# A decoder layer on one core: the down-projection as seven block products, and the first norm's scale and shift applied to h^T per partition

## The chip, the core and the metric

The kernel runs on one core of a Trainium2 chip. The metric is the device time of one execution in microseconds. Engines are named as in the profile: PE is TensorE, DVE VectorE, ACT ScalarE, POOL GpSimd, SP the engine that issues most of the loads.

## What is computed

One layer of a hybrid decoder over 1024 tokens of width 1024 (float32): a token mixer (a state-space group and a sparse-attention group), an output projection, a first layer norm, a channel mixer, a second layer norm. The part that matters here:

```
h = layer_norm(alpha * x + m, ln1_g, ln1_b)        # m: mixer output after its projection
u = causal_dwconv(h @ w_up, conv_w, conv_b)        # w_up 1024 x 5632, width 3
gate, up = split(u, 2)
f = (silu(gate) * up) @ w_down                     # w_down 2816 x 1024
out = layer_norm(alpha * h + f, ln2_g, ln2_b)
```

## The kernel before, in words

Every product is made of three matmuls (`three`, lines 156 to 159): each operand is split into an upper half (a copy rounded to the fp32r type) and a lower half (the rest), and upper x upper, upper x lower and lower x upper are added in one PSUM bank. The upper half is made by ACT, the lower one by POOL or DVE as `operand - upper` (`split`, lines 125 to 130).

The order on each engine but SP is set by the scheduler of the language, which simulates the program and takes, among the instructions that it expects to be ready, the one that stands first in the text; the engines then run these orders strictly. SP's order is the text's own (line 1134). Buffers are shared by tags with fixed counts (line 73): `wr` 3 (raw weights), `wh` and `wl` 3 each, `t4` 18, `wo` 8, `pp` 8, `pt` 3, `tx` 3; PSUM banks by the tags `ip` 2, `lg` 3, `tp` 2, `pv` 1 (line 75).

*First norm, lines 939 to 976.* For each of 8 token blocks r is loaded (a `pt` buffer), the last part of the output projection is added from PSUM, and `layer_norm` (lines 758 to 773) normalizes it. For the first six blocks (`LNP`, line 42) ACT normalizes, POOL multiplies by the scale (line 766) and DVE adds the shift (767); for the other two DVE does both in four steps (771, 772). The result goes to `h_dr` and is transposed by PE, eight 128 x 128 tiles per block (964). `put` (913 to 918) splits the transposed tile from PSUM into operands of the up-projection: `h11`, `h21` for tokens 0 to 511, `h22`, `t1`, `t2` for tokens 512 to 1023, later `t3`, `t4` (1008 to 1015). The t are differences of blocks of h^T.

*Up-projection, lines 1032 to 1064.* For each of `NF` = 22 column blocks j, seven block products (a Strassen-Winograd scheme over two column blocks, gate and up, two halves of the inner dimension and two halves of the tokens) of 12 matmuls each. `w_prep` (990 to 1005) makes the seven weight operands of the next j: four DVE sums, seven upper halves on ACT, seven lower halves on POOL (1003). Then the convolution (1058 to 1061), Silu and the product of gate and up, and the result goes to `g_dr` (1064).

*Down-projection, lines 1067 to 1109.* For each half of the tokens, eight PSUM banks hold 4 token blocks x 2 column halves. For each of the 22 row blocks k of w_down, `prep` (1074) loads 128 x 1024 of w_down (line 149) and 128 x 512 of g (1079), splits them (ACT 129 and 1080, POOL 130, DVE 1081), and 24 matmuls follow. The last 3 or 4 row blocks (`TAILS`) are run block by block, so that the second norm of one block (DVE, 1108 and `layer_norm`) lies beside the matmuls of the next.

## Time and profile before

| | |
|---|---|
| median of 3 runs | 1762.61 us (1762.0 to 1763.98) |
| profiled execution | 1762.1 us, its span 1760.2 us |
| PE busy in the span | 1622.6 us (92%), 7976 matmuls and transposes |
| DVE, ACT, POOL busy | 1245.4, 841.3, 803.9 us |
| mean granted clock of PE | 0.972 of full speed |
| first norm, up-projection, down-projection | about 1000 to 1085, 1085 to 1501, 1509 to 1760 us |

A busy time is the sum of the instructions' durations on an engine; an instruction's duration includes what it waits for after it has started. PE's matmuls overlap in the records: their pace is read from their starts. Times in rows count from the start of the span.

### The profile page before, as it was taken

What the parts mean: (1) busy time and instruction counts of PE and PEld (TensorE: products, weight loads), DVE (VectorE), ACT (ScalarE), POOL (GpSimd) and SP (SyncE); (2) the same over time, 40 slices, a digit from 0 to 9 for tenths busy, and PEclk for the clock granted to TensorE, in tenths of its full rate; (3) what the DMA queues carried; (4) which work ended last, traced back from release to release, by engine and by line L of the source; (5) the groups of instructions that cost most, each with busy time, mean ns of one, the idle gap of its engine ahead of it and who ended that gap; (6) DMA issues with size and microseconds to landing.
All of it is one profiled execution on the core that took longest, in us unless ns stands there. A gap on an engine that the chain in (4) does not pass through costs nothing.

```text
span 1760.2 us, 22843 instructions
## 1 busy us (share of the span) xinstructions
PE 1622.6 (92%) x7976; PEld 1342.8 (76%) x7976; DVE 1245.4 (71%) x2289; ACT 841.3 (48%) x1495; POOL 803.9 (46%) x560
## 2 busy tenths in 40 slices
PE   7899977888998989999999885999999999899998
PEld 6788866766887767778888764888888888688886
DVE  3534799998689667777787479888788786515516
ACT  3243474676411466666676344444444443333231
POOL 3223224453355443545464357765555553445351
PEclk9999999998999999999999997999999999899999
DMA  5122122123332473545454451322222223446443
GB/s 166 50 67 66 53 64 65 61 78 90 117 96 75 144 216 102 162 133 142 131 160 151 149 171 57 96 85 84 85 84 84 90 74 112 136 147 232 155 147 128
DMA packets 180937, 198.21 MB, mean 113 GB/s; under 512 B 12003, under 2 KB 136279, under 8 KB 180823
## 3 DMA queue, kind: packets, MB, share of 16 engines
q1 hardware_dynamic: 147351, 145.37, 28.0%
q10 hardware_dynamic: 33472, 51.39, 8.0%
q8 instruction: 63, 1.03, 0.3%
q14 instruction: 51, 0.42, 0.1%
HBM read 145.28 MB, written 51.45 MB: 112 GB/s over the span
## 4 chain that ended last, share of the span: by engine, by line
PE 44%; DVE 6%; DMA 2%; ACT 2%; issue 1%; POOL 1%; SPq 0%; DVEq 0%; ACTq 0%; POOLq 0%
PE acc L157 5%; PE acc L158 5%; PE acc L159 4%; PE pc L157 2%; PE pd L157 2%; PE pd L158 2%; PE pc L158 2%; PE pa L157 2%; PE pd L159 2%; PE pc L159 2%; PE ops L158 2%; PE ops L157 2%; PE ops L159 2%; PE pa L158 2%; PE pa L159 2%; PE ptp L695 2%
## 5 line engine op out<-in xcount | busy, mean ns | idle before, releaser
L130 POOL TENSOR_TENSOR w_lo<-w_raw,w_hi 128x1024 fp32r<-128x1024 f32 (+1 forms) x89 | 221.9, 2499 | 162.5 <-ACT w_hi L129 160.2
L157 PE MATMUL proj<-xTh,w_hi 128*128 128x512 f32 (+1 forms) x432 | 175.5, 407 | 30.2 <-DVE conv L483 10.4
L158 PE MATMUL proj<-xTl,w_hi 128*128 128x512 f32 (+1 forms) x432 | 173.7, 402 | 0.0
L159 PE MATMUL proj<-xTh,w_lo 128*128 128x512 f32 (+1 forms) x432 | 172.9, 401 | 0.0
L1003 POOL TENSOR_TENSOR w_hl<-s,w_hl 128x512 fp32r<-128x512 f32 x88 | 129.5, 1476 | 81.2 <-ACT w_hl L1002 80.8
L689 POOL TENSOR_SCALAR prob<-prob,sm 128x512 f32<-128x512 f32 (+7 forms) x128 | 97.5, 772 | 144.6 <-DVE sm L688 114.0
L1081 DVE TENSOR_TENSOR g_hl<-g_raw,g_hl 128x512 fp32r<-128x512 f32 x44 | 59.3, 1354 | 133.7 <-ACT g_hl L1080 129.3
L1003 POOL TENSOR_TENSOR w_hl<-w_raw,w_hl 128x512 fp32r<-128x512 f32 x66 | 106.3, 1613 | 88.9 <-ACT w_hl L1002 58.5
L157 PE MATMUL acc<-w_hi,g_hl 128*128 128x512 f32 x352 | 136.3, 395 | 7.8 <-ACT g_hl L1080 7.8
L158 PE MATMUL acc<-w_lo,g_hl 128*128 128x512 f32 x352 | 137.5, 391 | 0.0
L159 PE MATMUL acc<-w_hi,g_hl 128*128 128x512 f32 x352 | 137.4, 390 | 0.0
L127 POOL TENSOR_SCALAR w_hi<-w_raw 128x1024 fp32r<-128x1024 f32 x35 | 40.8, 1167 | 185.2 <-PE proj L158 153.6
L157 PEld LDWEIGHTS proj<-xTh,w_hi 128*128 128x128 f32 (+1 forms) x432 | 83.5, 193 | 50.6 <-issue 30.5
L686 ACT ACTIVATE prob<-prob,mx 128x512 f32<-128x512 f32 (+7 forms) x128 | 98.5, 771 | 39.2 <-DVE mx L683 36.0
L697 ACT ACTIVATE pt<-ptp 128x512 fp32r<-128x512 f32 x144 | 81.2, 594 | 65.4 <-PE ptp L695 44.6
L698 DVE TENSOR_TENSOR pt<-ptp,pt 128x512 fp32r<-128x512 f32 x144 | 95.5, 685 | 15.5 <-ACT pt L697 15.2
L157 PE MATMUL ops<-w_hi,y_hi 128*128 128x512 f32 x256 | 102.4, 401 | 4.1 <-ACT y_hi L129 3.1
L157 PE MATMUL tps<-w_hi,xTh 128*128 128x256 f32 x320 | 95.9, 301 | 9.6 <-ACT tout L617 6.9
L353 ACT ACTIVATE junk<-score,cand 128x1024 bf16<-128x1024 f32 (+2 forms) x96 | 86.1, 897 | 35.8 <-DVE cand L367 26.1
L158 PE MATMUL ops<-w_lo,y_hi 128*128 128x512 f32 x256 | 101.4, 396 | 0.4 <-DVE w_lo L130 0.4
L159 PE MATMUL ops<-w_hi,y_lo 128*128 128x512 f32 x256 | 100.5, 397 | 0.4 <-POOL y_lo L130 0.4
L129 ACT ACTIVATE w_hi<-w_raw 128x1024 fp32r<-128x1024 f32 (+1 forms) x62 | 65.2, 1052 | 74.0 <-PE acc L159 53.2
(315 smaller groups left out, 4793.3 us busy)
## 6 DMA issues: line engine op xcount, KB each, us to landing
w_raw<-in_ffn_w_up_dram SPq DMA_DIRECT2D x44, 512.0 KB, 3.9
w_raw<-in_ffn_w_down_dram SPq DMA_DIRECT2D x44, 512.0 KB, 3.7
w_raw<-in_w_in_dram SPq DMA_DIRECT2D x36, 512.0 KB, 4.1
r_dr<-rout ACTq DMA_DIRECT2D x48, 256.0 KB, 2.1
g_dr<-vg ACTq DMA_DIRECT2D x22, 512.0 KB, 2.6
g_raw<-g_dr SPq DMA_DIRECT2D x44, 256.0 KB, 4.0
acsb<-a_dr SPq DMA_DIRECT2D x16, 512.0 KB, 4.1
w_raw<-in_w_out_dram SPq DMA_DIRECT2D x16, 512.0 KB, 4.2
```

The lines of the kernel that those rows point to most:

```text
L129: nc.scalar.activation(hi, raw, AF.Copy)
L130: (nc.vector if lo_on_dve else nc.gpsimd).tensor_tensor(lo, raw, f(hi), op=OP.subtract)
L157: nc.tensor.matmul(ps, ah, bh, start=start, stop=False, skip_group_check=onto)
L158: nc.tensor.matmul(ps, ah, bl, start=False, stop=False, skip_group_check=onto)
L159: nc.tensor.matmul(ps, al, bh, start=False, stop=stop, skip_group_check=onto)
L353: nc.scalar.activation(junk[1][:, :n], score_ap[b], AF.Sign, bias=c, scale=-1.0, accum_out=val[e][:, i:i + 1])
L686: nc.scalar.activation(t[:, :w], t[:, :w], AF.Exp, bias=mx[:, h:h + 1], scale=-1.0, accum_out=sm[:, h:h + 1])
L689: nc.gpsimd.tensor_scalar(t[:, :w], t[:, :w], sm[:, 4 + h:5 + h], 1.0, op0=OP.mult, op1=OP.mult)
L697: nc.scalar.activation(pt[:, 0], ps, AF.Copy)
L698: nc.vector.tensor_tensor(pt[:, 1], ps, f(pt[:, 0]), op=OP.subtract)
L1003: nc.gpsimd.tensor_tensor(t[:, 1], src, f(t[:, 0]), op=OP.subtract)
L1081: nc.vector.tensor_tensor(t[:, 1], raw, f(t[:, 0]), op=OP.subtract)
```

## The change

The first norm leaves out scale and shift in the row layout: DVE normalizes r in one `tensor_scalar`, the bare result goes to `h_dr` in one store and is transposed, and ACT applies scale and shift on the way out of PSUM, where the width lies on the partitions (`column`, 8 activations of 128 x 128 per block, with the two vectors as columns 176 to 191 of `fw`). `put` and the differences then read this SBUF tile. The lower halves of `h21` and `h22` go from DVE to POOL. In `w_prep` two of seven lower halves go from POOL to DVE.

The down-projection becomes seven block products over two halves of the tokens, of the row blocks and of the columns. The 22 steps of the up-projection are taken in pairs (row block j//2 of either half); after the second of a pair DVE makes four combinations of g, and seven blocks are stored per pair where two rows of two blocks were. The seven products P1, P2, P6, P7, P4, P5, P3 follow, each over 11 row blocks with 12 matmuls, on one of two sets of four PSUM banks. Operands of w_down are combined on DVE (P6, P4, P5); lower halves of weights are made on POOL, those of g on DVE. `h_dr` is loaded ahead of P2 and of P7, four blocks each, and POOL applies scale and shift there (`first_norm`).

```diff
+g_dr = dram.tile([NF // 2 * P, 7, 512], F32)             # was [DFF, L]
-g1, b1 = ln_consts(ln1_g, ln1_b)                          # ahead of the first norm
+for i, v in enumerate((ln1_g, ln1_b)):
+    nc.sync.dma_start(frow[1][48 + 8 * i:56 + 8 * i], ...)
+def column(dst, ps, k4):
+    for k in range(4):
+        kk = k4 * 4 + k
+        nc.scalar.activation(dst[:, k * P:(k + 1) * P], ps[:, k * P:(k + 1) * P], AF.Identity,
+                             bias=fw[:, 184 + kk:185 + kk], scale=fw[:, 176 + kk:177 + kk])
-        layer_norm(r, g1, b1, i < LNP, lambda ns: nc.scalar.dma_start(h_dr[bs, ns], r[:, ns]))
+        layer_norm_stats(r, D, mv[:, 0:2])
...
+        nc.vector.tensor_scalar(r, r, mv[:, 0:1], mv[:, 2:3], op0=OP.subtract, op1=OP.mult)
+        nc.scalar.dma_start(h_dr[bs, :], r)
...
+            hr = h_raw[b][:, k4] if b < 4 else mid("hr")
+            column(hr, ps, k4)
             if b < 4:
-                put((h11, h21)[k4], k4n(ps), o, nc.vector)
-                nc.scalar.activation(h_raw[b][:, k4], ps, AF.Copy)
+                put((h11, h21)[k4], k4n(hr), o, (nc.vector, nc.gpsimd)[k4])
             elif k4 == 0:
-                nc.vector.tensor_tensor(d1, ps, h_raw[b - 4][:, 0], op=OP.subtract)
+                nc.vector.tensor_tensor(d1, hr, h_raw[b - 4][:, 0], op=OP.subtract)
                 put(t1, k4n(d1), o, nc.gpsimd)
             else:
-                nc.vector.tensor_tensor(d2, ps, d1, op=OP.subtract)
-                put(h22, k4n(ps), o, nc.vector)
+                nc.vector.tensor_tensor(d2, hr, d1, op=OP.subtract)
                 put(t2, k4n(d2), o, nc.vector)
+                put(h22, k4n(hr), o, nc.gpsimd)
...
-            nc.gpsimd.tensor_tensor(t[:, 1], src, f(t[:, 0]), op=OP.subtract)        # w_prep
+            lo_eng = nc.vector if len(out) in (2, 5) else nc.gpsimd
+            lo_eng.tensor_tensor(t[:, 1], src, f(t[:, 0]), op=OP.subtract)
...
-        nc.scalar.dma_start(g_dr[j * P:(j + 1) * P, :], vg)
+        if j % 2 == 0:
+            v1 = vg
+            nc.scalar.dma_start(g_dr[rows, 0], v1[:, :512])
+        else:
+            nc.scalar.dma_start(g_dr[rows, 1:3].rearrange("p a n -> p (a n)"), vg)
+            q13, q24 = x_tile("q13"), x_tile("q24")
+            nc.vector.tensor_tensor(q13[:, :512], v1[:, 512:], vg[:, 512:], op=OP.add)
+            nc.vector.tensor_tensor(q24[:, :512], q13[:, :512], v1[:, :512], op=OP.subtract)
+            nc.vector.tensor_tensor(q13[:, 512:], v1[:, :512], v1[:, 512:], op=OP.subtract)
+            nc.scalar.dma_start(g_dr[rows, 3:5].rearrange("p a n -> p (a n)"), q13)
+            nc.vector.tensor_tensor(q24[:, 512:], vg[:, :512], q24[:, :512], op=OP.subtract)
+            nc.scalar.dma_start(g_dr[rows, 5:7].rearrange("p a n -> p (a n)"), q24)
...
+def first_norm(r):
+    nc.gpsimd.tensor_tensor(r, r, g1, op=OP.mult)
+    nc.gpsimd.tensor_tensor(r, r, b1, op=OP.add)
+def right(p, k):
+    if p == "P1":
+        keep[k] = w_row(k, 0, 1024, "t4")                  # stays until P4
+        return keep[k][:, :512]
+    if p == "P2":
+        return w_row(KT + k, 0, 512, "wr")
+    if p == "P6":                                          # two sums
+        raw = w_row(KT + k, 512, 512, "wr")
+        nc.vector.tensor_tensor(keep[k][:, 512:], raw, keep[k][:, 512:], op=OP.subtract)
+        nc.vector.tensor_tensor(keep[k][:, :512], keep[k][:, 512:], keep[k][:, :512], op=OP.add)
+        return keep[k][:, :512]
+    if p == "P7":
+        return keep[k][:, 512:]
...
+def prep(p, k):
+    raw = big("g_raw", tag="pt", shape=(P, 512))
+    nc.sync.dma_start(raw, g_dr[k * P:(k + 1) * P, LEFT[p]])
+    w_raw = right(p, k)
+    gt = big("g_hl", F32R, (P, 2, 512), "pp")
+    nc.scalar.activation(gt[:, 0], raw, AF.Copy)
+    nc.vector.tensor_tensor(gt[:, 1], raw, f(gt[:, 0]), op=OP.subtract)
+    wt = big("wd_hl", F32R, (P, 2, 512), "t4" if p == "P3" else WDTAG[n_prep[0] % 2])   # wh, wl
+    nc.scalar.activation(wt[:, 0], w_raw, AF.Copy)
+    nc.gpsimd.tensor_tensor(wt[:, 1], w_raw, f(wt[:, 0]), op=OP.subtract)
...
+run("P1", pa, False)
+for t in range(4):
+    nc.scalar.activation(c1[t], pa[t], AF.Copy)
+r1 = h_rows(0)                                             # 4 loads, 4 first_norm
+run("P2", pa, True)
...
+run("P6", pb, False)
...
+r2 = h_rows(1)
+run("P7", pa, False)
...
+run("P4", pa, True)
...
+run("P5", pb, False)
+for t in range(4):
+    nc.vector.tensor_tensor(r2[t][:, N2], r2[t][:, N2], pb[t], op=OP.add)
+    last_norm(r2[t], 4 + t)
+run("P3", pb, True, 6, finish_tile)                        # last 6 k token block by token block
```

P4 and P5 subtract one operand of w_down each (11 DVE operations of 512 columns); P5 loads rows of 1024 columns again. After P2, P7 and P4 DVE adds the banks to r1 and r2.

## Rows read from the trace of the kernel before

**Rows 1.** Stretches: us, busy us (instructions) by engine, PEclk, DMA share, GB/s.

```profile
1000.00:1052.00 52.00, 47.35 (x218) 38.32 (x217) 36.42 (x69) 24.49 (x43) 25.66 (x12) 0.97 0.49 163
1052.00:1085.00 33.00, 11.63 (x46) 8.07 (x45) 32.19 (x49) 14.85 (x41) 20.67 (x17) 0.68 0.24 80
...
1102.00:1501.00 399.00, 398.11 (x1754) 328.52 (x1753) 316.13 (x292) 179.41 (x245) 214.26 (x141) 1.00 0.27 88
...
1509.30:1751.10 241.80, 241.79 (x1056) 199.94 (x1056) 98.69 (x113) 73.93 (x94) 109.49 (x44) 0.99 0.50 167
1751.10:1760.20 9.10, 0.34 (x2) 0.00 (x0) 6.10 (x12) 0.29 (x1) 0.00 (x0) 0.63 0.30 115
```

**Rows 2.** The chain that ended last, in order of time: start us, us, what.

```profile
1034.47 5.65 DMA r<-r_dr
...
1052.30 0.45 PE hTp L964 x4
...
1084.42 0.77 PE pb L158
...
1507.69 1.04 ACT w_hi L129
```

**Rows 3.** Timeline of PE around 1500 us: start us, us, instruction [idle before].

```profile
1499.04 0.39 PE L159 MATMUL pd<-h22h,w_hl 128*128 128x512 f32 x1
...
1501.08 0.39 PE L159 MATMUL pd<-h22h,w_hl 128*128 128x512 f32 x1
...
1509.31 3.78 PE L157 MATMUL acc<-w_hi,g_hl 128*128 128x512 f32 x8 [7.84 <-ACT g_hl L1080]
...
1514.16 0.58 PE L159 MATMUL acc<-w_hi,g_hl 128*128 128x512 f32 x1
```

**Rows 4.** Timeline at 1524 us, POOL and DVE.

```profile
1524.18 2.39 POOL L130 TENSOR_TENSOR w_lo<-w_raw,w_hi 128x1024 fp32r<-128x1024 f32 x1 [3.05 <-ACT w_hi L129]
...
1526.15 0.97 DVE L1081 TENSOR_TENSOR g_hl<-g_raw,g_hl 128x512 fp32r<-128x512 f32 x1 [3.56 <-ACT g_hl L1080]
```

**Rows 5.** Groups by shape, POOL: count, busy us, mean ns, idle before.

```profile
L766 POOL TENSOR_TENSOR r<-r,ln_g 128x1024 f32<-128x1024 f32 x6 | 14.4, 2395 | 15.2 <-ACT r L765 15.2
...
L918 POOL TENSOR_TENSOR t4l<-d,t4h 128x256 fp32r<-128x256 f32 x8 | 7.3, 944 | 0.0
```

**Rows 6.** Line 1003 alone: count, shortest, median and longest in ns.

```profile
L1003 POOL TENSOR_TENSOR w_hl<-s,w_hl x88: 1285/1301/2288, 1058.9 to 1476.9; 128x512 fp32r<-128x512 f32 x88
```

**Rows 7.** DMA issues of the down-projection: KB each, median us to landing.

```profile
w_raw<-in_ffn_w_down_dram SPq DMA_DIRECT2D x41, 512.0 KB, 3.7
g_raw<-g_dr SPq DMA_DIRECT2D x41, 256.0 KB, 4.0
r<-h_dr SPq DMA_DIRECT2D x8, 512.0 KB, 6.2
```

**Rows 8.** Groups by shape, DVE.

```profile
L996 DVE TENSOR_TENSOR s<-w_raw 128x512 f32<-128x512 f32 x22 | 17.7, 804 | 0.0
...
L772 DVE SCALAR_TENSOR_TENSOR r<-r,lnmv,ln_b 128x512 f32<-128x512 f32 x20 | 17.3, 901 | 0.1
...
L771 DVE SCALAR_TENSOR_TENSOR r<-r,lnmv,ln_g 128x512 f32<-128x512 f32 x20 | 15.0, 792 | 0.2
...
L767 DVE TENSOR_TENSOR r<-r,ln_b 128x1024 f32<-128x1024 f32 x6 | 7.3, 1218 | 0.0
...
L918 DVE TENSOR_TENSOR t2l<-t2raw,t2h 128x256 fp32r<-128x256 f32 x8 | 6.8, 880 | 0.0
...
L918 DVE TENSOR_TENSOR h11l<-hTp,h11h 128x256 fp32r<-128x256 f32 x8 | 3.3, 416 | 1.0 <-ACT h11h L917 0.9
...
L310 DVE TENSOR_SCALAR score<-relu,wq 128x1024 f32<-128x1024 f32 x1 | 0.8, 752 | 0.0
```

**Rows 9.** Six stretches of 19 us in the up-projection, together.

```profile
sum 114.00, PE 114.00 PEld 94.36 DVE 92.81 ACT 52.17 POOL 72.30; mean PE 19.00 PEld 15.73 DVE 15.47 ACT 8.70 POOL 12.05
```

**Rows 10.** Groups by shape, ACT.

```profile
L765 ACT ACTIVATE r<-r,lnmv 128x1024 f32<-128x1024 f32 x6 | 7.4, 1241 | 3.7 <-DVE lnmv L764 2.7 <-ACT lnmv L761 1.0
...
L278 ACT ACTIVATE dtset<-acsps 128x128 f32<-128x128 f32 x1 | 0.3, 278 | 0.0
```

## What the change was predicted to do

> **What bounds the kernel now.** I read the stretches first [rows 1]. From 1102 to 1501 us (up-projection) PE is busy 398.1 of 399 us, from 1509.3 to 1751.1 us (down-projection) 241.8 of 241.8, both at the full granted clock: there a matmul more or less is its own price. Three places are not PE-bound: 1052 to 1085 us (end of the first norm), where PE works 11.6 of 33 us, DVE 32.2 and the clock falls to 0.68; a gap between the two projections; and 9.1 us after the last matmul. The chain in order of time [rows 2] says what ends each. A block's r arrives 5.65 us after its issue; from the transposes at 1052.3 us all is DVE work until PE restarts on t2's lower half at 1084.4. Between the projections PE waits 7.84 us for ACT's first upper half of w_down, issued only at 1507.7, behind the last Silu. The timeline gives PE's pace [rows 3]: nine matmuls in 2.04 us, 0.2267 us each; and after the 7.84 us gap the first eight take 3.78 us and the pace stays low until about 1514, some 2.5 us lost. One collision shows a resource that no busy share shows [rows 4]: POOL's subtraction ends at 1526.57; a DVE subtraction that started at 1526.15 ends at 1527.12, 0.55 us behind it. DVE and POOL do not read two SBUF operands at once. I call 0.55 us per 512 columns what such a DVE operation takes of this shared path; a POOL operation takes its whole length.
>
> **Down-projection, PE.** Before, 22 row blocks x 8 token blocks x 2 column halves x 3 = 1056 matmuls; after, 7 products x 11 x 4 x 3 = 924. 132 x 0.2267 = **-29.9 us**; PE then needs 209.5.
>
> **Down-projection, what feeds it.** Before, the shared path carried 44 x (2.40 + 0.55) = 130 of 241.8 us [rows 4, 1]. After: 77 lower halves of weights on POOL x 1.28 [rows 6] = 98.6; 8 reloaded blocks of h, each scaled and shifted on POOL, 16 x 2.40 [rows 5] = 38.3; 77 lower halves of g x 0.55 = 42.4; the combinations of w_down, 22 in P6, 11 in P4, 11 in P5, x 0.55 = 24.2; 12 additions to r and 16 steps of the second norm of four blocks x 0.55 = 15.4. Sum 219 us, more than PE's 209.5; and some 12 us of the last 72 matmuls must follow the last lower half. So about 231, or 22 behind PE, if the path never rests.
>
> By stages: P1 asks 11 x 1.83 = 20 of its 29.9 us. The loads of h stand in SP's queue behind P1's loads and ahead of P2's, and take 6.2 us to land [rows 7], so about 20 us into P1 POOL begins 8 x 2.40 = 19.2 us of scaling and shifting that the program text puts ahead of P2's lower halves. P2's first lower half comes at about 40 us; PE can run the two products that need no lower half of w for the three raw buffers only, 24 x 0.2267 = 5.4 us past 29.9: idle 5 to 8. The same burst before P7 meets six finished weight tiles (10.9 us of cover): idle 5 to 9. P6 asks 11 x (1.28 + 3 x 0.55) = 32.2, P4 32.8 with the additions behind u3: 2 to 3 each. P5 has 26.2 of 29.9. With hand-overs where a bank is read before the next product adds to it (u3, the second r tiles, 0.68 us each) I take **+24 us**, beside the 22 of the account; bounds 4 (the path mostly overlaps) and 46 (both bursts bare). Weight and g loads of 512 and 256 KB land in 3.7 and 4.0 us [rows 7] and have a lead of three buffers: nothing, unless P1 and P5 (768 KB per 2.72 us) lose it.
>
> **The gap and the end.** j = 21 is odd: four more DVE combinations, its vu waits for a tx buffer, and two more stores sit in ACT's queue waiting for DVE, in front of P1's first halves: **+3** (-4 to +6). At the end a token block costs DVE an addition, two statistics and four steps, seven operations over 512 columns at about 0.7 (the steps 0.6 to 0.9 [rows 8]), some 5 us, against 18 matmuls or 4.1: **+1.5** (0 to 4).
>
> **Up-projection.** DVE is busy 15.47 of 19.0 us per step [rows 9]. It gets two lower halves of weights and on average two combinations, 4 x 0.6 = 2.4: 17.9, odd steps 19.1, even 16.7. The shared path: before 7 x 1.28 + 14 x 0.55 = 16.7, after 5 x 1.28 + 18 x 0.55 = 16.3. PE hides it, with eight and more us of lead in the weights; but u3 and xu must leave PSUM within one product (2.7 us) behind longer DVE work: **+3** (0 to 12). Stores grow from 1.0 to 1.8 MB per pair of steps, on a DMA share of 0.27 [rows 1]: nothing.
>
> **First norm.** DVE loses six shifts of 1.22, eight steps of about 0.85, sixteen lower halves of 0.41 (h21, h22, to POOL): 20.7 us. It gets eight tensor_scalar over 1024 columns, between 0.75 (L310, one SBUF operand) and 1.22 (L767, two); the first is its form: 6.0. The lower halves of h11 and the differences d1, d2 now read SBUF instead of PSUM. The rows tell the price: h11l 0.416 us from PSUM, t2l 0.880 from SBUF, same size, same stretch [rows 8]: 16 x 0.46 = 7.4. Two lower halves of weights: 1.6. Net -5.7 us of DVE. A block's norm shrinks from 1.24 on ACT + 2.40 on POOL + 1.22 on DVE to 0.75, so its r buffer (three for eight blocks) returns some 4 us sooner, and DVE's idle 13.7 us before 1052 [rows 1] fill up, a third of them say. ACT gets 64 columns x 0.28 [rows 10] = 17.8 and loses eight copies and six scalings of 1.24, together about 12, on a share under one half [rows 1]; POOL loses 14.4 and gets sixteen lower halves of 0.95 [rows 5]. **-10 us**, bounds -20 and +4. The vectors' loads move: two small ones on SP here, two broadcasts to SP ahead of P1, in buffers freed by then: nothing.
>
> The Trainium skill (SBUF — State Buffer, Who interferes with whom) says that a vector operation with at most one SBUF input stays clear of GpSimd, while one with two SBUF inputs takes turns with it. By that rule alone the change trades 16 immune operations for exposed ones, up to a whole POOL operation each; the trace agrees in kind, 0.88 against 0.42 us. The skill (VectorE: DVE Perf Modes, The perf-mode tier table) gives fp32 tensor_scalar twice the rate of tensor_tensor; by its 1227 ns for 2048 elements an estimate for eight is 5 us instead of 6.0, and the stage would come out 1 us shorter.
>
> **Sum.** -29.9 + 24 + 3 + 1.5 + 3 - 10 = -8.4. The profiled execution took 1762.1 us (span 1760.2 and 1.9 around it): 1753.7. It lies 0.5 below the median 1762.6, so **1754**.
>
> **Rivals.** *The path does not bind*: POOL and DVE interleave as in the up-projection, where 16.7 of 19.0 us cost PE nothing [rows 9], and the bursts fall into P1's slack; stalls 4 instead of 24: 1734. Against it: 219 is more than PE's time. *Nothing moves*: the stalls reach 30 to 36 and eat the products saved and the norm's gain together; the norm's scaling only changed its place, and 38.3 us on POOL replace 14.4: about 1762. *Slower*: both bursts lie bare. If the h tiles land at the end of P1 and of P6 and not 10 us before, POOL starts 19.2 us of work when PE has 5.4 and 10.9 of cover; with the two excesses of P6 and P4 and restarts at half clock [rows 3] stalls are 46: 1776. It decides from 32 us of stalls on. For it: POOL's queue is in order and the text puts the scaling first. *DVE bounds the up-projection*: odd steps at 19.1 plus waits cannot borrow from even ones, 11 x 0.9 = 10 more, to 1764; it adds to the case of no change.
>
> **Chances.** Forecast 0.47, path free 0.18, no change (with the DVE case) 0.14, slower 0.21. A measurement here tells about 0.2%, 3.5 us, from no change. Faster 0.65, same 0.14, slower 0.21. The range goes from the free path to just short of the bare bursts: 1732 to 1771; the forecast's own is 1740 to 1758.
>
> **What would show it.** Right: 924 matmuls on the accumulators; POOL and DVE together near 219 us of shared work in the stage; PE idle behind the eight scalings before P2 and P7; PE's restart on t2 some 10 us earlier; up-projection still 398 of 399. Wrong: PE without idle in P2 and P7 (then 1734), or idle of over 32 us in the stage, or a DVE wait in front of the matmuls of the up-projection.

## The result: slower by 1.5%, 38 us above the forecast

The changed kernel takes 1791.96 us (median of 4 runs, 1788.88 to 1793.28), the kernel before on the same chip 1763.3; the ratio is 1.0154, 95% interval 1.0137 to 1.0170. The forecast was 1754, its range 1732 to 1771. The profiled execution has a span of 1791.6 us against 1760.2.

The same stretches as in [rows 1], for the changed kernel: us, busy us (instructions) by engine, PEclk, DMA share, GB/s.

```profile
1052.00:1085.00 33.00, 15.12 (x54) 10.81 (x51) 31.57 (x34) 21.75 (x61) 29.82 (x25) 0.76 0.17 56
...
1102.00:1508.60 406.60, 398.84 (x1737) 324.09 (x1735) 348.46 (x366) 175.10 (x242) 157.08 (x98) 1.00 0.30 100
1508.60:1527.00 18.40, 0.39 (x3) 0.05 (x1) 10.42 (x11) 4.69 (x5) 0.02 (x1) 0.61 0.40 143
1527.00:1779.00 252.00, 222.92 (x924) 180.36 (x924) 187.19 (x202) 95.45 (x163) 153.84 (x93) 0.93 0.59 194
1779.00:1791.60 12.60, 0.34 (x2) 0.00 (x0) 9.42 (x19) 0.59 (x2) 0.00 (x0) 0.63 0.33 125
```

PE has its 924 matmuls in the down-projection and needs 252.0 us for them, 42.5 more than 924 x 0.2267. Of these 42.5 us PE is idle for 29.1; the other 13.4 are its slower pace after waits (busy 222.92, not 209.5, at a mean granted clock of 0.93). The gap ahead has grown from 8.2 to 18.4 us, the up-projection from 401.7 to 413.2 (from its 84th matmul on, which is defined below), the tail from 9.2 to 12.6. The end of the first norm is as full of DVE work as before (31.57 of 33 us), POOL is now busy 29.82 of 33.

Where PE stood in the down-projection (timeline of PE: start us, us, instruction, idle before and what ended it):

```profile
1567.60 0.79 PE L157 MATMUL acc<-wd_hl,g_hl 128*128 128x512 f32 x1 [6.96 <-POOL wd_hl L1154]
...
1626.65 0.79 PE L157 MATMUL acc<-wd_hl,g_hl 128*128 128x512 f32 x1 [3.58 <-POOL wd_hl L1154]
...
1636.69 0.50 PE L157 MATMUL acc<-wd_hl,g_hl 128*128 128x512 f32 x1 [2.87 <-POOL wd_hl L1154]
1641.15 0.50 PE L157 MATMUL acc<-wd_hl,g_hl 128*128 128x512 f32 x1 [2.35 <-POOL wd_hl L1154]
...
1679.98 0.76 PE L156 MATMUL acc<-wd_hl,g_hl 128*128 128x512 f32 x1 [6.91 <-ACT wd_hl L1153]
...
1746.90 0.80 PE L156 MATMUL acc<-wd_hl,g_hl 128*128 128x512 f32 x1 [5.25 <-DVE r L1219]
```

The first is P2's first lower half, the next three fall at the end of P6 and the beginning of P7, the fifth is the start of P4, the last the start of P3. After a wait of 3.6 us or more a matmul shows 0.76 to 0.80 us. The stretches of P2 and P6, which hold such waits, have a mean clock of 0.91 and 31.8 and 33.1 us of PE time (rows under rows_apart); products without one have 1.00 and 29.92 (rows under swap).

POOL and DVE at the start of P2, to be read beside [rows 4] (timeline of the changed kernel):

```profile
1550.51 4.75 POOL L1105 TENSOR_TENSOR r<-r,ln_g 128x1024 f32<-128x1024 f32 x2
...
1556.19 7.94 DVE L1151 TENSOR_TENSOR g_hl<-g_raw,g_hl 128x512 fp32r<-128x512 f32 x3 [0.39 <-ACT g_hl L1150]
1558.02 5.56 POOL L1105 TENSOR_TENSOR r<-r,ln_g 128x1024 f32<-128x1024 f32 x2
...
1566.29 2.49 POOL L1154 TENSOR_TENSOR wd_hl<-wd_raw,wd_hl 128x512 fp32r<-128x512 f32 x2
```

P2's first lower half starts at 1566.29, behind six of the eight scaling operations, and beside them one DVE subtraction takes 7.94 / 3 = 2.65 us where it takes 0.69 alone: each waits for one POOL operation.

### The profile page after: what moved, and what is told of

It reads as the page before. It is cut to its first block, busy times and chain, and to the rows that moved or that the text cites. A ratio compares the mean times of both kernels' runs of the same rounds, so it can differ in the third digit from the quotient of the medians.

```text
span 1791.6 us, 23113 instructions
## 1 busy us (share of the span) xinstructions
PE 1608.8 (90%) x7844; PEld 1323.0 (74%) x7844; DVE 1373.7 (77%) x2446; ACT 871.3 (49%) x1615; POOL 787.8 (44%) x575
## 4 chain that ended last, share of the span: by engine, by line
PE 41%; DVE 34%; DMA 11%; issue 6%; ACT 4%; POOL 3%; SPq 1%; DVEq 0%; ACTq 0%; POOLq 0%
DVE junk L349 4%; PE proj L156 4%; PE proj L157 4%; PE proj L158 4%; DMA wd_raw<-in_ffn_w_down_dram 3%; PE ops L156 3%; PE ops L158 3%; PE ops L157 3%; DVE vu L1080 3%; DVE lmat L528 3%; PE ptp L694 2%; DVE vg L1080 2%; DMA w_raw<-in_ffn_w_up_dram 2%; PE pv L700 2%; PE pv L699 2%
## 5 line engine op out<-in xcount | busy, mean ns | idle before, releaser
L1022 POOL TENSOR_TENSOR w_hl<-s,w_hl 128x512 fp32r<-128x512 f32 x88 | 137.3, 1571 | 178.6 <-ACT w_hl L1020 178.6
L1154 POOL TENSOR_TENSOR wd_hl<-wd_raw,wd_hl 128x512 fp32r<-128x512 f32 x77 | 111.7, 1459 | 120.2 <-ACT wd_hl L1153 118.1
L156 PE MATMUL acc<-wd_hl,g_hl 128*128 128x512 f32 x308 | 116.7, 407 | 30.9 <-ACT wd_hl L1153 24.9
L1151 DVE TENSOR_TENSOR g_hl<-g_raw,g_hl 128x512 fp32r<-128x512 f32 x77 | 95.5, 1250 | 61.0 <-ACT g_hl L1150 60.8
L157 PE MATMUL acc<-wd_hl,g_hl 128*128 128x512 f32 x308 | 124.7, 405 | 16.2 <-POOL wd_hl L1154 16.2
L129 POOL TENSOR_TENSOR w_lo<-w_raw,w_hi 128x1024 fp32r<-128x1024 f32 (+1 forms) x45 | 111.9, 2490 | 26.0 <-ACT w_hi L128 23.8
L158 PE MATMUL acc<-wd_hl,g_hl 128*128 128x512 f32 x308 | 123.3, 401 | 0.0
L697 DVE TENSOR_TENSOR pt<-ptp,pt 128x512 fp32r<-128x512 f32 x144 | 95.5, 685 | 15.6 <-ACT pt L696 15.3
L157 PE MATMUL tps<-w_lo,xTh 128*128 128x256 f32 x320 | 96.0, 301 | 3.9 <-POOL w_lo L129 3.9
```

Of the source, the lines that this page charges most:

```text
L129: (nc.vector if lo_on_dve else nc.gpsimd).tensor_tensor(lo, raw, f(hi), op=OP.subtract)
L156: nc.tensor.matmul(ps, ah, bh, start=start, stop=False, skip_group_check=onto)
L157: nc.tensor.matmul(ps, ah, bl, start=False, stop=False, skip_group_check=onto)
L158: nc.tensor.matmul(ps, al, bh, start=False, stop=stop, skip_group_check=onto)
L697: nc.vector.tensor_tensor(pt[:, 1], ps, f(pt[:, 0]), op=OP.subtract)
L1022: lo_eng.tensor_tensor(t[:, 1], src, f(t[:, 0]), op=OP.subtract)
```

## The experiments

All stretches below come from the profiled executions, in us, by the starts of PE's matmuls. "84th" is the start of the up-projection's 84th matmul (a step j has 84), and tells when the first norm lets PE go on; "up" goes from there to the up-projection's last matmul, "gap" from that to the first of the down-projection (negative where it begins earlier), "down" to its last matmul, "tail" to the end of the span. The 84th lies between 1093.4 and 1097.3 in the nine kernels whose program is the changed one up to there, so a difference of 2 or 3 us in one cell says little.

Some of the expectations below go by another mark, DVE's eviction of `pd` into `xg` in the first step: a first step that ended at 1092.6 or 1102.1 us, up-projections of 399 to 406 us. That mark is not the same point of the work in every kernel. When it came, PE had begun 94 matmuls of the up-projection in the kernel before, 113 in the changed kernel and 92 in norm_alone, lo_pool and lo_first, because the order between the first and the second step differs. So 21 matmuls, 4.8 us, of what looks like a later end of the first norm in the changed kernel is work that the others did afterwards.

| kernel | median us | ratio to before, 95% | 84th | up | gap | down | tail |
|---|---|---|---|---|---|---|---|
| before | 1763.3 | | 1099.3 | 401.7 | 8.2 | 241.7 | 9.2 |
| changed | 1792.0 | 1.0154 (1.0137 to 1.0170) | 1095.4 | 413.2 | 18.4 | 252.0 | 12.6 |
| no_scaling | 1768.8 | 1.0027 (1.0017 to 1.0037) | 1095.7 | 412.4 | 18.5 | 228.1 | 11.7 |
| spread | 1797.8 | 1.0192 (1.0172 to 1.0212) | 1097.3 | 411.7 | 18.4 | 263.4 | 11.7 |
| rows_apart | 1787.2 | 1.0123 (1.0108 to 1.0139) | 1093.4 | 412.5 | 18.6 | 249.5 | 11.9 |
| one_operand | 1781.6 | 1.0098 (1.0080 to 1.0117) | 1093.7 | 411.6 | 18.6 | 241.6 | 14.2 |
| swap | 1789.3 | 1.0133 (1.0117 to 1.0149) | 1096.7 | 412.4 | 18.7 | 246.0 | 14.8 |
| vec_late | 1792.4 | 1.0155 (1.0140 to 1.0170) | 1097.1 | 412.1 | 13.7 | 257.8 | 11.7 |
| early_prep | 1782.3 | 1.0093 (1.0080 to 1.0107) | 1094.3 | 415.8 | -8.8 | 267.1 | 11.7 |
| norm_alone | 1757.1 | 0.9953 (0.9938 to 0.9968) | 1090.6 | 403.9 | 8.2 | 241.8 | 9.6 |
| old_norm | 1775.7 | 1.0060 (1.0044 to 1.0077) | 1099.1 | 411.8 | 14.2 | 232.0 | 11.6 |
| lo_pool | 1806.6 | 1.0236 (1.0219 to 1.0252) | 1094.6 | 432.9 | 18.3 | 253.0 | 11.7 |
| lo_first | 1789.7 | 1.0138 (1.0121 to 1.0154) | 1091.6 | 411.8 | 18.7 | 253.2 | 12.8 |
| no_combos | 1773.2 | 1.0046 (1.0029 to 1.0063) | 1096.6 | 401.4 | 10.1 | 251.9 | 11.8 |
| best_rows | 1787.0 | 1.0123 (1.0106 to 1.0141) | 1092.1 | 432.8 | -5.9 | 254.9 | 14.7 |
| best_old | 1780.6 | 1.0087 (1.0073 to 1.0102) | 1101.3 | 437.2 | -8.6 | 236.1 | 13.9 |
| best2_rows | 1775.3 | 1.0066 (1.0051 to 1.0080) | 1089.6 | 417.4 | -5.9 | 252.0 | 19.0 |
| best2_old | 1764.4 | 0.9994 (0.9983 to 1.0004) | 1101.4 | 415.9 | -8.8 | 234.3 | 19.3 |
| norm_rescaled | 1759.7 | 0.9967 (0.9955 to 0.9978) | 1093.5 | 405.6 | 10.1 | 245.6 | 9.2 |
| norm_early | 1752.3 | 0.9931 (0.9917 to 0.9944) | 1087.9 | 407.5 | -7.7 | 255.0 | 9.2 |

### What the scaling of h costs in the down-projection

**no_scaling.**

```diff
-            first_norm(r)
```

> This kernel is the changed one with the 16 GpSimd operations that scale and shift the reloaded rows of h left out of the down-projection (the output then lacks the first norm's scale and shift in the residual). Theory A, the two bursts lie bare: the stalls of P2 (21 us) and P7 (7.5 us) go, those of P6, P4 and P5 (13 us) stay: 25 to 28 us less than the changed kernel, about 1766. Theory B, the sum of the shared path binds: 38 us of 219 go, the rest fits into PE's 209, all 43 us of stalls go: about 1750. Theory C, the stalls come from loads that arrive late: no change, 1792.

The down-projection falls from 252.0 to 228.1 us and the median by 23.2, nearest to theory A: PE's idle time in P2 and at P7 is gone. The stalls that stay, 228.1 - 209.5 = 18.6 us, stand at the starts of P1, P4 and P3 and not in P6 or P5. (Stretches of no_scaling, P2 and P6.)

```profile
1558.30:1588.22 29.92, 29.92 (x134) 24.77 (x132) 21.28 (x22) 16.16 (x28) 17.50 (x13) 1.00 0.71 230
1588.22:1619.09 30.87, 30.22 (x134) 24.70 (x133) 25.94 (x29) 12.00 (x21) 14.75 (x10) 1.00 0.60 195
```

**spread.**

```diff
-    r1 = h_rows(0)
+            if p in ("P1", "P6") and k == 2:
+                h_rows(("P1", "P6").index(p))
+            if k % 2 == 0 and later:
+                r, v, op = later.pop(0)
+                nc.gpsimd.tensor_tensor(r, r, v, op=op)
```

> All work is kept; the 16 GpSimd operations are issued one to every second row block, from the third block of P1 and of P6 on, instead of eight in a row ahead of P2 and P7. Theory A (bursts): P2 and P7 lose their stalls nearly as if the operations were gone, 18 to 25 us less than the changed kernel, 1767 to 1774. Theory B (sum of the shared path): the sum is the same 219 us, so the time stays within 5 us of 1792. Theory C (loads): 1792.

None of the theories: 6 us slower than the changed kernel. The trace shows why: the scheduler had put six of the eight operations in a row again, as soon as the rows were there, now into P1, which has no finished weight tiles to run on. The first 132 matmuls took 49.4 us (31.4 in the changed kernel), those of P6 49.3. So this run moved the bursts instead of spreading them, and says only that they cost more where there is less cover. (Stretches of spread, columns as above.)

```profile
1527.34:1576.74 49.40, 35.47 (x132) 27.94 (x132) 29.32 (x17) 20.07 (x34) 44.03 (x24) 0.81 0.76 268
```

**rows_apart.**

```diff
+    AT = {("P1", 2): 0, ("P1", 6): 1, ("P1", 10): 2, ("P2", 3): 3,
+          ("P6", 2): 4, ("P6", 6): 5, ("P6", 10): 6, ("P7", 3): 7}
+            r = big("r2", tag="wo")
+            nc.sync.dma_start(r, h_dr[AT[p, k] * P:(AT[p, k] + 1) * P, :])
+            first_norm(r)
```

> All work is kept; the eight rows of h are now loaded one at a time, four row blocks apart (P1 at its 3rd, 7th and 11th, P2 at its 4th, the same in P6 and P7), and each row's two GpSimd operations stand behind its load in the queue, so that no more than two of them follow each other. Theory A (bursts in GpSimd's queue are what costs): most of the 23 us that leaving the operations out saved come back, 15 to 23 less than the changed kernel, 1769 to 1777. Theory B (the sum of work on the path shared by DVE and GpSimd binds): the sum is unchanged, the time stays within 5 us of 1792.

5 us less, nearer to B. P2 loses its stall, P6 gets it. The stretches of 132 matmuls of P2 and P6 in the changed kernel:

```profile
1558.32:1597.75 39.43, 31.75 (x132) 25.38 (x130) 23.32 (x20) 16.60 (x28) 31.97 (x19) 0.91 0.55 174
1597.75:1637.26 39.51, 33.06 (x133) 26.52 (x132) 33.63 (x34) 14.56 (x25) 26.73 (x15) 0.91 0.53 169
```

and in rows_apart:

```profile
1558.57:1589.03 30.46, 30.23 (x133) 24.70 (x132) 17.84 (x17) 14.12 (x24) 23.62 (x14) 1.00 0.74 235
1589.03:1632.08 43.05, 34.68 (x134) 26.19 (x132) 41.48 (x33) 14.79 (x26) 34.58 (x17) 0.92 0.49 156
```

P2 now holds only two of the 16 operations, and they fit in: 30.46 us. P1 holds six and takes 34.2 us, 2.6 more than in no_scaling; P6 holds seven and takes 12.2 more. In P1 a row block asks DVE for one operation, in P6 for three, and there DVE is busy 41.48 of 43.05 us. So neither theory alone: where DVE has slack the burst is a matter of order, in P6 there is no slack to spread it over.

**one_operand.**

```diff
-        nc.gpsimd.tensor_tensor(r, r, g1, op=OP.mult)
-        nc.gpsimd.tensor_tensor(r, r, b1, op=OP.add)
+        for c in (2.0, 0.5, 2.0, 0.5):
+            nc.gpsimd.tensor_scalar(r, r, c, 1.0, op0=OP.mult, op1=OP.mult)
```

> The changed kernel with each of the 16 GpSimd operations that scale and shift h (two SBUF operands, 2.40 us alone) replaced by two tensor_scalar operations on the same tile (one SBUF operand, about 1.15 us each alone by the rows of the kernel before), so GpSimd's queue is as long as it was, and the scale and shift are left out of the residual. Theory, queue: the stalls are the time that P2's and P6's lower halves wait behind the scaling in GpSimd's queue, so the time stays within 6 us of the changed kernel, 1786 to 1792. Rival, path: DVE and GpSimd exclude each other only where both read two SBUF operands, DVE now runs beside the scaling, and most of the 23 us of the bursts go: 1770 to 1778. In between, the share tells how much of the bursts is queue and how much path.

In between: 10.3 of the 23.2 us come back, with 40.4 us on POOL for the 32 new operations where the 16 old ones took 42.9. But it isn't the second operand (POOL and DVE of one_operand ahead of P2):

```profile
1547.58 10.05 POOL L1106 TENSOR_SCALAR r<-r 128x1024 f32<-128x1024 f32 x9
...
1552.00 2.68 DVE L1151 TENSOR_TENSOR g_hl<-g_raw,g_hl 128x512 fp32r<-128x512 f32 x2 [6.16 <-ACT g_hl L1150]
```

Beside POOL operations with one SBUF operand of 1.12 us each, a DVE subtraction takes 1.34 us, again twice its time alone. DVE still waits for one POOL operation per operation of its own; that operation is only half as long. That the pieces' length makes the 10 us is argued from these rows; shorter pieces also let lower halves in earlier, and the run doesn't separate the two.

### The hand-overs and the gap

**swap.**

```diff
-    run("P4", pa, True)
-    for t in range(4):
-        nc.vector.tensor_tensor(r2[t][:, N1], r2[t][:, N1], pa[t], op=OP.add)
     run("P5", pb, False)
+    for t in range(4):
+        nc.vector.tensor_tensor(r2[t][:, N2], r2[t][:, N2], pb[t], op=OP.add)
+    run("P4", pa, True)
```

> The changed kernel with P5 computed before P4: then no product adds onto banks that the product just before it has filled and that DVE has still to read (P7 to P4, P5 to P3). Theory: the stalls at the start of P4 (7 us and a restart at half clock) and of P3 (5.4 us and a restart) are bank hand-overs behind other DVE work, and go: 10 to 16 less than the changed kernel, 1776 to 1782. Rival: they are P4's weight loads and combinations that come late, as the trace names them (ACT's upper half of w_down): they stay wherever P4 stands, no change beyond 5 us.

The total gains 2.7 us only, but the stall at P4 is gone: the 132 matmuls of P5 and of P4 run at 29.92 us each (stretches of swap: P5, P4, P3),

```profile
1672.81:1702.73 29.92, 29.92 (x134) 24.77 (x132) 26.92 (x30) 12.15 (x20) 16.44 (x11) 1.00 0.78 248
1702.73:1732.65 29.92, 29.92 (x134) 24.77 (x132) 22.17 (x25) 13.94 (x23) 17.30 (x12) 1.00 0.63 200
1732.65:1773.16 40.51, 33.98 (x133) 26.27 (x132) 33.90 (x57) 12.06 (x23) 11.57 (x9) 0.87 0.40 138
```

where P4 and P5 took 38.4 and 29.9 in the changed kernel. P3 is 2.8 us longer and the tail 2.2, because the second norms of four blocks now stand in DVE's queue ahead of P3's last lower halves. So the trace's label at P4, "ACT wd_hl", named the wrong releaser: the upper half that ACT ended just before is that of P4's sixth row block, and the first had long been there. DVE's timeline in the changed kernel has the right one:

```profile
1672.99 0.68 DVE L1132 TENSOR_TENSOR wd_raw<-wd_raw 128x512 f32<-128x512 f32 x1
...
1677.47 1.77 DVE L1132 TENSOR_TENSOR wd_raw<-wd_raw 128x512 f32<-128x512 f32 x1
1679.16 0.68 DVE L1204 TENSOR_TENSOR cu<-uu,acc 128x512 f32<-128x512 f32 x1
...
1744.92 1.33 DVE L1151 TENSOR_TENSOR g_hl<-g_raw,g_hl 128x512 fp32r<-128x512 f32 x1 [1.19 <-ACT g_hl L1150]
1746.17 0.68 DVE L1219 TENSOR_TENSOR r<-r,acc 128x512 f32<-128x512 f32 x1
```

P7's last matmul is at 1672.7; the addition that reads its bank (L1204) is ready then, but stands behind combinations and lower halves of P4's operands that wait for loads, and ends at 1679.84; PE goes on at 1679.98. At P3 the same with L1219, behind a lower half that waited for ACT.

**vec_late.**

```diff
-    g2, b2 = ln_consts(ln2_g, ln2_b); g1, b1 = ln_consts(ln1_g, ln1_b)
     run("P1", pa, False)
+    g2, b2 = ln_consts(ln2_g, ln2_b); g1, b1 = ln_consts(ln1_g, ln1_b)
```

> The changed kernel with the four broadcast loads of the norms' vectors issued after P1 instead of ahead of it; they took four buffers that were free early, and P1's first w_down row block took one that waits for the store of the last gated block. Theory: that block then lands early and PE starts the down-projection at about 1523 instead of 1527, when ACT gets past the stores of the last combinations: 4 us less, 1788. Rival: the buffers given out are no earlier, or the vectors come late for the scaling: no change or some us more.

The gap shrinks by 4.7 us, where 4 were expected, and the down-projection gives 5.8 back (P1 and P2 are 3.3 and 2 us longer; that the vectors' later loads are why was not shown). Median unchanged.

**early_prep.**

```diff
         if j + 1 < NF:
             ws[j + 1] = w_prep(j + 1)
+        else:
+            early = [prep("P1", k) for k in range(5)]
...
+            if p == "P1" and k == 6:
+                g_store(rows, stores)
```

`g_store` issues the last three stores; the vectors' loads stand behind P1 as in vec_late.

> The changed kernel with the operands of P1's first five row blocks issued ahead of the last conv, the three last stores issued after them, and the vectors' loads after P1. Theory: the 18 us between the last matmul of the up-projection and the first of the down-projection are queue order (P1's first loads and upper halves stand behind the last stores) and shrink to 2 to 6 us: 10 to 16 less than the changed kernel, 1776 to 1782. Rival: the last conv and the combinations then come later on DVE and ACT and P1 stalls at its sixth block by what was gained: within 4 us of 1792.

9.7 us less. P1 begins before the up-projection has ended (gap -8.8) and has stalls in its middle, as the rival said, but keeps a third of what it gained (27.2 of gap against 15.1 of down and 2.6 of up). So the gap itself is queue order, but most of what it held comes back behind it. The rows of the changed kernel (SP's and ACT's queues and ACT):

```profile
1505.87 0.33 SPq L1147 DMA_DIRECT2D g_raw<-g_dr  x1
...
1518.98 0.33 ACTq L1088 DMA_DIRECT2D g_dr<-vg  x1
...
1521.15 0.33 ACTq L1095 DMA_DIRECT2D g_dr<-q  x1
1521.53 0.63 ACT L1150 ACTIVATE g_hl<-g_raw 128x512 fp32r<-128x512 f32 x1 [5.60 <-DVE q L1094]
...
1521.67 0.33 SPq L1111 DMA_DIRECT2D wd_raw<-in_ffn_w_down_dram  x1
```

SP stands from 1505.87 to 1521.67 in front of P1's first load of w_down (in vec_late this load is issued at 1506.69). That its buffer held the last gated block until the store issued at 1518.98 had landed is read from the order in which buffers are given out, the trace doesn't name it. ACT makes P1's first upper half of g at 1521.53, behind the last store.

### The first norm and the up-projection

**norm_alone.** The kernel before with the first norm of the change (lines 945 to 994), rows of h stored bare.

```diff
-        layer_norm(r, g1, b1, i < LNP, lambda ns: nc.scalar.dma_start(h_dr[bs, ns], r[:, ns]))
+        nc.vector.tensor_scalar(r, r, mv[:, 0:1], mv[:, 2:3], op0=OP.subtract, op1=OP.mult)
+        nc.scalar.dma_start(h_dr[bs, :], r)
...
+            column(hr, ps, k4)
```

> The kernel before with the new first norm alone (the rows of h stored without scale and shift, which the residual then lacks). Prediction's term: 10 us less than before, ratio 0.994. Rival: the transposes end earlier but the lower halves of t1, t2 and the weights on DVE and GpSimd take it back by the end of the first up-projection step: ratio 0.999 to 1.001.

8.3 us less by the ratio. PE's 84th matmul comes 8.7 us sooner, and the up-projection takes 2.2 us of it back. The prediction's -10 has 1.6 us for two lower halves in it that this kernel doesn't move; without them it said -11.6.

**old_norm.**

```diff
-        nc.vector.tensor_scalar(r, r, mv[:, 0:1], mv[:, 2:3], op0=OP.subtract, op1=OP.mult)
-        nc.scalar.dma_start(h_dr[bs, :], r)
+        layer_norm(r, g1, b1, i < LNP, lambda ns: nc.scalar.dma_start(h_dr[bs, ns], r[:, ns]))
...
-            first_norm(r)
```

> The changed kernel with the first norm as it was before: scale and shift on the token rows, finished rows stored, no scaling in the down-projection. Theory A: the new norm is worth nothing by the end of the first up-projection step, so this equals the kernel without scaling, about 1766 (within 3 us of it). Rival: the new norm is worth the 10 us of the prediction, so this is 10 us above the kernel without scaling, about 1776.

By the medians 6.9 us above no_scaling, between the two; in the profiled executions 2.1 (84th +3.4, up -0.6, gap -4.3, down +3.9); the profiled one is the fastest of old_norm's four. At its own place the new norm brings 3.4 us beside the rest of the change, where it brings 8.7 alone: something else in the stage takes more than half of its gain. Why the gap and the down-projection differ is open.

**lo_pool.**

```diff
-            lo_eng = nc.vector if len(out) in (2, 5) else nc.gpsimd
+            lo_eng = nc.gpsimd
```

> The changed kernel with all seven lower halves of w_up's operands on GpSimd again (the change had moved two of seven to DVE). Theory: with the new norm alone the first up-projection step ended at 1092.6 us, in the changed kernel at 1102.1, and DVE's extra lower halves are what stands between; they also delay u3 and xu in the later steps. The step ends at 1092 to 1095, the up-projection loses some of its 7 us of stalls: 9 to 15 less than the changed kernel, 1777 to 1783. Rival: the stage is lost to something else in the order, and GpSimd now stands in DVE's way in the up-projection: the first step still ends at 1100 to 1104, no change or up to 5 us more.

The theory was right for the first norm, though not in size, and wrong for the up-projection, which loses 19.7 us where it was to gain some. From the last block's transposes to DVE's eviction into `xg` (stretches of norm_alone, of the changed kernel and of lo_pool):

```profile
1061.22:1092.63 31.41, 24.16 (x86) 18.98 (x87) 25.93 (x26) 18.11 (x46) 30.35 (x27) 0.84 0.16 51
```

```profile
1062.30:1102.14 39.84, 29.11 (x107) 23.04 (x108) 34.82 (x35) 19.50 (x49) 33.52 (x29) 0.83 0.21 66
```

```profile
1065.21:1096.61 31.40, 24.46 (x86) 18.92 (x87) 25.94 (x27) 18.10 (x47) 30.34 (x27) 0.84 0.16 51
```

31.4 us with all lower halves on POOL, 39.8 with two of seven on DVE; but PE has 107 instructions in the second stretch and 86 in the others, and 21 matmuls more are 4.8 of the 8.4 us. What is lost is PE's waiting (PE of the changed kernel, then of lo_pool):

```profile
1082.33 0.55 PE L156 MATMUL pc<-t3h,w_hl 128*128 128x512 f32 x1 [3.63 <-ACT t3h L918]
1085.83 0.79 PE L157 MATMUL pc<-t3l,w_hl 128*128 128x512 f32 x1 [2.94 <-DVE t3l L919]
```

```profile
1084.05 0.50 PE L156 MATMUL pc<-t3h,w_hl 128*128 128x512 f32 x1 [2.34 <-ACT t3h L918]
1085.13 0.51 PE L157 MATMUL pc<-t3l,w_hl 128*128 128x512 f32 x1 [0.58 <-DVE t3l L919]
```

6.57 against 2.92 us, and from the last block's transposes to the 84th matmul it is 33.1 against 29.4: 3.7 us. In DVE's queue of the changed kernel two such halves and the sums for the next step stand ahead of the last halves of t3 (DVE's timeline):

```profile
1075.95 1.23 DVE L1022 TENSOR_TENSOR w_hl<-w_raw,w_hl 128x512 fp32r<-128x512 f32 x1
...
1081.39 0.69 DVE L1022 TENSOR_TENSOR w_hl<-w_raw,w_hl 128x512 fp32r<-128x512 f32 x1
...
1084.83 1.81 DVE L919 TENSOR_TENSOR t3l<-d,t3h 128x256 fp32r<-128x256 f32 x2
```

In the up-projection the same move does the opposite, 432.9 us against 413.2; PE's waits there, changed kernel, lo_pool and no_combos, which comes below (engine, line, releaser: us in total, times, longest):

```profile
PE pd L156 <- DVE xu L1068: 4.0, 9, 1.3
PE pc L156 <- DVE u L1065: 3.5, 6, 1.5
```

```profile
PE pc L156 <- DVE u L1064: 11.4, 9, 1.8
PE pd L156 <- DVE xu L1067: 8.8, 6, 1.9
```

```profile
PE pc L156 <- DVE u L1065: 0.9, 2, 0.6
```

**lo_first.**

```diff
+            lo_eng = nc.vector if j > 1 and len(out) in (2, 5) else nc.gpsimd
```

> The changed kernel with all lower halves of w_up on GpSimd for the first two steps alone (the two weight sets that are prepared while the first norm ends), two of seven on DVE from the third on. Theory: with all on GpSimd the first step ended 8.6 us sooner after the last transpose and the later steps took 24 us longer; these are separate, so the first step ends at 1092 to 1095, the up-projection stays at 406 us, and 8 to 9 us come off: 1782 to 1785. Rival: the slower start of the later steps takes the gain back: within 3 us of 1792.

The 84th matmul comes 3.8 us sooner (3.7 in lo_pool, counted from the transposes), the up-projection takes 1.4 less and the rest of the profile 1.7 more; the median falls by 2.3. The number is the rival's, its reason is not: the later steps take nothing back. The 8 to 9 us of the theory were the mark's, and about 4 are what the two halves cost at this place.

**no_combos.**

```diff
-            nc.vector.tensor_tensor(q13[:, :512], v1[:, 512:], vg[:, 512:], op=OP.add)
-            nc.vector.tensor_tensor(q24[:, :512], q13[:, :512], v1[:, :512], op=OP.subtract)
-            nc.vector.tensor_tensor(q13[:, 512:], v1[:, :512], v1[:, 512:], op=OP.subtract)
-            nc.vector.tensor_tensor(q24[:, 512:], vg[:, :512], q24[:, :512], op=OP.subtract)
```

> The changed kernel with the four DVE combinations of g in each odd step left out and the same bytes stored from the two gated blocks themselves (the products then multiply other data; two of the ten temporary buffers of a pair of steps go with them). Theory: the 7 us of stalls in the up-projection and a part of the gap come from these operations in DVE's queue: the up-projection goes from 406 back to 399 to 401, the gap from 18 to 15: 8 to 11 less, 1781 to 1784. Rival: the stalls come from the two lower halves on DVE or from the larger stores: the up-projection stays at 405 to 407.

18.8 us less, twice the theory: the up-projection falls by 11.8, to that of the kernel before, and the gap by 8.3 (two temporary buffers per pair of steps go with the operations, so a part may be theirs). With lo_pool this makes a table of four, the up-projection in us:

| | lower halves all on POOL | two of seven on DVE |
|---|---|---|
| no combinations | 401.7 (before, with smaller stores) | 401.4 (no_combos) |
| four combinations in odd steps | 432.9 (lo_pool) | 413.2 (changed) |

The combinations cost 12 us where DVE makes two lower halves, 31 where it doesn't (29 against norm_alone). So the moved halves, which cost the first norm about 4 us and the up-projection nothing by themselves, save 20 where the combinations are. Why they do is not shown.

### Versions built from these

**best_rows** (lo_pool, early_prep, swap, the second half's norms spread over P3, and the rows of h scaled one by one, three of them in POOL's idle time before P1) and **best_old** (the same with the old norm and finished rows). In best_rows, and in best2_rows below, the raw weights from P2 on also take the eight `wo` buffers, because the rows of h lie in `wr`.

```diff
+        if j + 1 == NF:
+            r1 = [h_row(t, "wr") for t in range(3)]
...
+    AT = {("P1", 4): 3, ("P2", 1): 4, ("P2", 7): 5, ("P7", 0): 6, ("P7", 6): 7}
...
+            if p == "P3" and k in (1, 3, 5, 7):
+                last_norm(r2[k // 2], 4 + k // 2)
```

> The changed kernel with five edits: all lower halves of w_up on GpSimd, P1's first five row blocks and late stores as in the early preparation, P5 before P4, the four norms of the second half spread over P3, and the scaling of three rows of h in GpSimd's idle time before P1, of the others one by one in P1, P2 and P7. Theory (the losses are separate and queue order causes most): 9 to 15, 10, 9 and 8 to 15 us come off 1792, so 1743 to 1756, below the kernel before (1766). Rival (the path shared by DVE and GpSimd is full wherever work is put): no better than the best single edit, 1775 to 1782.

> As the one before, but with the old first norm and finished rows of h, so no scaling in the down-projection at all: 1776 less about 10 for the early preparation, 9 for P5 before P4 and the spread norms, and 0 to 5 in the up-projection: 1752 to 1757. If the new norm is worth its 8 us in the end and its scaling can be hidden, this one is slower than the one with rows scaled; if the scaling can't be hidden, faster.

Both missed: they carry lo_pool's 20 us in the up-projection (432.8 and 437.2).

**best2_rows** (lo_first in place of lo_pool) and **best2_old** (the changed kernel's split), both with ACT and POOL in the norms of P3.

```diff
+            lo_eng = nc.vector if j > 1 and len(out) in (2, 5) else nc.gpsimd
...
+                last_norm(r2[k // 2], 4 + k // 2, True)
```

> Changed kernel, new norm; lower halves on GpSimd in the first two steps alone; P1's first five row blocks and the late stores as in the early preparation; P5 before P4; the second half's four norms with ACT and GpSimd in place of two of DVE's passes; the scaling of the rows of h placed in idle time of GpSimd where there is any. Theory: the up-projection ends at about 1502 (1508 less 8.6 and some us for the early operands), the rest takes 249 us as with these products before, less 8 in P3, and a tail of 12: about 1755. Rival: the path is full, 1765 or more.

> The same with the old first norm and finished rows of h (nothing to scale later), two of seven lower halves on DVE throughout: up-projection to 1512, the rest 227 less 8 in P3, tail 12: about 1745 to 1750. If the path shared by DVE and GpSimd is what the seven products fill, this one beats the one with rows scaled by 5 us or more although its norm is 8 us slower.

best2_old beats best2_rows by 11 us, as the path's theory said; the two also differ in the split of the lower halves and in the buffers of the raw weights. In the profiles its 84th matmul comes 11.8 us later and its down-projection is 17.7 shorter. Both missed their numbers, by 14 to 20 us, in the up-projection's end (5), the down-projection (5 to 7) and the tail (7; in best2_old DVE waits 2.93 us for POOL's scaling in the second half's norms, and the last four norms stand behind that in its queue). With every repair found, seven products come out where the kernel before is: 0.9994, 0.9983 to 1.0004. One of these repairs, operands issued ahead of the last conv, is worth some 7 us to the old product too (norm_early against norm_rescaled, below). Whether another order would win is open.

**norm_rescaled** and **norm_early**: the kernel before with the new norm, POOL scaling four rows in the middle of each half of the old down-projection; then also the operands of its first two row blocks ahead of the last conv.

```diff
+            if k in (5, 8, 11, 14):
+                nc.sync.dma_start(r, h_dr[bb * P:(bb + 1) * P, :])
+                nc.gpsimd.tensor_tensor(r, r, g1, op=OP.mult)
+                nc.gpsimd.tensor_tensor(r, r, b1, op=OP.add)
...
+        else:
+            for k in range(2):
+                prep(k, 0, wk0, gk0)
```

> The kernel before with the new first norm, and the scale and shift of the reloaded rows of h on GpSimd in the middle of each half of the old down-projection (four rows, three row blocks apart). Theory: the old down-projection asks 130 us of 242 of the path of DVE and GpSimd, 38 more fit: the norm's 8 to 9 us stay, about 1757, ratio 0.994 to 0.997. Rival: the bursts cost there too: ratio 1.000 or above.

> The kernel before with the new first norm, the rows of h scaled inside the old down-projection, and the operands of the down-projection's first two row blocks issued ahead of the last conv. Theory: the old gap of 8 us is queue order too (ACT's first half of w_down behind the last Silu) and two row blocks are 10.9 us of matmuls: 5 to 8 us less than the kernel with the rows scaled, 1752 to 1755, ratio 0.992 to 0.994. Rival: the operands delay the last conv and the third row block by as much: ratio 0.9967 as without.

Both as the theories said. norm_rescaled has ratio 0.9967 (0.9955 to 0.9978): where PE does 1056 matmuls, most of POOL's scaling hides. 5.8 us of norm_alone's 8.3 are left, with intervals that overlap; in the profiled execution, the slowest of its 12, the down-projection is 3.9 us longer than before. norm_early, which leaves nothing out, beats both kernels: 0.9931 (0.9917 to 0.9944), 12.5 us below the kernel before, whose median beside it was 1764.8.

## Why the prediction was wrong

The terms, with what the two profiled executions show (spans 1760.2 and 1791.6):

| term | predicted | measured |
|---|---|---|
| PE, 132 matmuls fewer | -29.9 | -29.9 |
| what feeds the down-projection | +24 (4 to 46) | +40.2 (252.0 - 241.7 + 29.9) |
| gap between the projections | +3 (-4 to +6) | +10.2 |
| tail | +1.5 (0 to 4) | +3.4 |
| up-projection | +3 (0 to 12) | +11.4 |
| first norm, by the 84th matmul | -10 (-20 to +4) | -4.0 |

**The step that failed most** is the term of +24 us. Its two parts that were mis-sized: the bursts, "idle 5 to 8" before P2 and "5 to 9" before P7, cost 23.9 (no_scaling), and the hand-overs, taken at 0.68 us each, left PE standing for 6.9 us at P4 and 5.3 at P3, with a restart behind each. The slower pace after waits, 13.4 us in the stage, has no place of its own in the +24; only the slower rival counts restarts. P6 cost what was said or less: without the scaling its 132 matmuls took 30.9 us.

The reason for the first is in how the path was counted. I added up what each operation takes of it (219 us) and compared sums. The rows show turns: beside a POOL operation of 2.78 us every DVE operation waits for one, so in a burst DVE falls to one operation per POOL operation. At the end of P6 and the beginning of P7 seven lower halves of g take DVE 15.40 us:

```profile
1626.24 15.40 DVE L1151 TENSOR_TENSOR g_hl<-g_raw,g_hl 128x512 fp32r<-128x512 f32 x7 [5.42 <-ACT g_hl L1150]
```

How much of the 23.9 us comes from these turns, and how much from the lower halves that wait in POOL's own queue, no run separates. The Trainium skill (SBUF — State Buffer, Who interferes with whom) says that a vector operation with two SBUF inputs contends with a GpSimd instruction that reads SBUF, and it exempts one with at most one SBUF input only outside the 2-port perf modes, a condition that the prediction left out; the trace agrees for two inputs, 2.65 us beside two-operand operations, 1.34 beside one-operand ones, 0.69 alone.

The reason for the second is the order on DVE: I priced the addition that frees a bank at its own length, and didn't ask what stands ahead of it in the queue. The scheduler had put P4's operands there, which wait for loads.

**The -10 of the first norm** was near for the norm alone (norm_alone: -8.7, where the sum without the lower halves says -11.6) and came out as -4.0 in the changed kernel. The term that failed is "two lower halves of weights: 1.6" us of DVE: in a stage where DVE is busy 31.57 of 33 us they and what is queued with them cost 3.7 (lo_pool; 3.8 in lo_first); the rest is within the 2 or 3 us by which the 84th matmul differs between equal programs. Two lesser prices were low too: the activation per 128 x 128 tile took 0.46 us and not 0.28, on an engine with room; the `tensor_scalar` 1.08 and not 0.75. The Trainium skill (VectorE: DVE Perf Modes, The perf-mode tier table) gives the latter twice the rate of `tensor_tensor`; beside POOL's work the mean here shows no more than the 1.22 us of a `tensor_tensor` of that size [rows 8] less a tenth. Groups by shape, changed kernel, 985 to 1110 us:

```profile
L949 ACT ACTIVATE hr<-hTp,fw 128x128 f32<-128x128 f32 x32 | 11.9, 461 | 3.3 <-DVE r L969 2.2 <-DVE r L974 1.0
...
L974 DVE TENSOR_SCALAR r<-r,lnmv 128x1024 f32<-128x1024 f32 x8 | 8.7, 1084 | 0.1
```

**The gap** came out beyond its bounds: "the vectors' loads ... in buffers freed by then: nothing" looked at the loads and not at the buffers that they take from P1. vec_late takes 4.7 us out of the gap, no_combos 8.3, of 10.2 that came with the change: 13.0 in sum, so the causes overlap.

**The up-projection**: the mechanism was right, PE waits for u3 and xu behind longer DVE work, and the size too small, +11.4 for +3. The combinations are the cause: without them, and the two buffers that go with them, the excess is gone (no_combos). **The tail** was right in kind. **PE's part** was exact: 29.92 us for 132 matmuls where nothing is late.

**Rivals.** The slower one came nearest: it named the bursts and put the stage's stalls at 46, measured 42.5; with the other terms as predicted that is 1770 to 1776. The other terms add 23.5 us: the up-projection 8.4, the gap 7.2, the norm 6.0, the tail 1.9. *DVE bounds the up-projection*, 10 us more, named the first of these. "Nothing moves" has best2_old's time only by coincidence: its stalls in the down-projection are 24.8 us and not 30 to 36.

**Two slips in the working**, neither of which moves the forecast far. DVE's idle time before 1052 us is 52.00 - 36.42 = 15.6 us by [rows 1]; 13.7 comes from the column of the weight loads. Six weight tiles of 12 matmuls cover 16.3 us and not 10.9, which would have made the burst before P7 look smaller still.

## What to carry to other kernels

Price a moved operation by what stands behind it in its engine's queue, not by its own length: two lower halves per step put on DVE cost about 4 us where it was full and saved 20 in the up-projection. Products saved on a busy PE are paid for by the engines that prepare them: here 29.9 us of matmuls bought combinations that cost about 20. An engine that is free in the stage where the work was (POOL beside 1056 matmuls) is not free where PE has less to do. Compare stages at equal work: by an eviction that stood behind PE's 92nd matmul in one kernel and behind its 113th in another, a loss of 3.7 us looked like 8.4.

## What was not expected of the hardware

- POOL's one-operand operations hold up DVE as the two-operand ones do, one for one; with pieces half as long the kernel was 10 us faster.
- An activation with scale and shift per partition took 0.46 us for 128 x 128 out of PSUM; a plain one in [rows 10] 0.28.
